# Row sums of x on TensorE, a root in halves, and single feature blocks at the head of a transformer block's kernel

## The chip, the cores and the metric

The kernel runs on one core of one Trainium2 chip. The metric is the device time of an execution in microseconds. Four executions of the kernel before are shown: three timed runs and the profiled one.

## The reference, cut to what matters

The reference computes one layer of a diffusion backbone over 256 latent tokens (x) and 256 context tokens (ctx) with 2048 features in float32. The part that matters here is its beginning:

```
mod   = silu(c) @ w_ada + b_ada            # 6 x 2048 columns, latent tokens
mod_c = silu(c_ctx) @ w_ada + b_ada        # the same for context tokens
h_lat = rmsnorm(x,   norm1_g) * (1 + sc1)  + sh1
h_ctx = rmsnorm(ctx, norm1_g) * (1 + csc1) + csh1
z     = h @ w_in                           # 8000 columns: attention q, k, v, MLA parts, gates
rmsnorm(x, g) = x * rsqrt(mean(x * x) + 1e-6) * g
lam   = exp(sum(lp[0] * lp[1])) - exp(sum(lp[2] * lp[3])) + 0.2   # used in the attention alone
```

Behind it come differential attention, multi-head latent attention, the merge of both, a SwiGLU feed-forward part and a last norm, which the change does not touch.

## The kernel before, in words

Tokens are the free dimension and features the partitions: `xnT` holds 16 k-tiles of 128 features by 512 tokens, latent tokens first. A float32 operand is split into a high part and a low part in the reduced type fp32r, written by ScalarE (a copy) and VectorE (the difference), and a product is three matmuls: high by high, high by low, low by high. In the names `hl` and `hc` stand for the modulated activations of latent and context tokens, `wh` and `wl` for weights, with two buffers each for the parts of an activation and three for each part of a weight.

**Row sums and root.** x arrives in eight units of two k-tiles. ScalarE squares a unit (L338, L341), VectorE adds it to `xsum` of 1024 columns (L342), folds that to 512 columns (L343), and TensorE multiplies by a matrix of ones (L345), which leaves each token's sum on every partition in `ps`. The function `newton` (from L323) makes the reciprocal root: Ln, Exp and Square on ScalarE (L325 to L327), a correction step of three operations on VectorE (L328 to L330). The result `rb` has a column for each token.

**Modulation, block by block.** `mod_gemv(f0, nf, order)` makes shift and scale of `nf` k-tiles from `f0` on. It first multiplies x by `rb` on VectorE (L388). Its weights `w_mod` are 2 MB a k-tile, in units of 512 KB (`sraw`, twelve buffers, L394). TensorE multiplies each of the 16 contraction tiles by 32 columns that hold c and c_ctx, four in different column groups at a time (L408, the "vector products" below; `pgb` is their bank), ScalarE copies the sums (L401), TensorE transposes them (L404), VectorE adds the four groups up (L415) and makes shift and scale (L421, L422, `modc`). Then ScalarE writes the high part of the modulated k-tile (L427), VectorE modulates in float32 (L428) and writes the low part (L429).

**First products.** `first_group` loads two parts of `w_in` for the same k-tiles (320 and 512 columns each, 832 in all; five buffers `raw`), splits them (L439 to L442, L169, L170), and puts 42 matmuls a k-tile into a list, `queue`: seven output groups by two streams by three parts. Their sums stay in seven banks (`g`, `g_x`) over all 16 k-tiles.

**The order.** TensorE's order in this stage is written by hand (`manual_schedule`). The list `order` of a call says it step by step: "g4" means four vector products, "t" the copy, eight products of the queue and the transposes, a number that many products of the queue. So the products of one block cover the vector products and the modulation of the next. The calls before are two single blocks (k-tiles 0 and 1) and seven pairs. The other engines take their work in the order of a scheduler. Weights and x come through SP's queue, in program order; the transfers share eight semaphores in turn, so each waits until the one eight places ahead (x, w_mod, w_in and the two small ones alike) has landed. The small vector operands and `da_lambda` come through ScalarE's queue. `da_lambda`'s two dot products, exponential and sum are made at the very start (L297 to L305).

Behind the stage the query, key and value projections begin, with the sums of the latent norm (L590) first.

Of the kernel before, what the change touches and what calls it, by code (L numbers as in the profile page):

```python
# [26 lines left out]
LAM_INIT = 0.8 - 0.6 * math.exp(-0.0)  # L27
# [69 lines left out]
def kernel(  # L97
# [19 lines left out]
    const, _c0 = pool("const")  # L117
    ctx.callback(_c0)
    stream, _c1 = pool("stream")
# [19 lines left out]
    def nm(s):  # L139
        uid[0] += 1  # L140
        return f"{s}{uid[0]}"
# [93 lines left out]
    def group_b(w, c0, n, nkt, toks, name, ups=2, tick=None, stagger=0):  # L235
# [41 lines left out]
    ones = const.tile([P, P], F32, name="ones")  # L277
# [10 lines left out]
    b1 = const.tile([P, 16], F32, name="b1")  # L288
    nc.vector.tensor_scalar_add(b1, bcol[:, 16:32], 1.0)

    ls = const.tile([P, 4], F32, name="ls")
    setup = stream.tile([P, 1024], F32, tag="wl", name="setup", bufs=3)
    lamb, lj = setup[:, 0:256], setup[:, 512:576]
    nc.scalar.dma_start(
        out=lamb, in_=da_lambda.rearrange("a f d -> (a f d)").partition_broadcast(P))
    for i in range(2):
        nc.vector.tensor_tensor_reduce(  # L297
            lj, lamb[:, i * 128 : i * 128 + 64], lamb[:, i * 128 + 64 : i * 128 + 128],
            op0=ALU.mult, op1=ALU.add, scale=1.0, scalar=0.0, accum_out=ls[:, i : i + 1])
    with tc.issue_after(silu.ins):  # L300
        nc.scalar.preload_act_table_set("natural_log_exp_and_others")
    nc.scalar.activation(ls[:, 0:2], ls[:, 0:2], AF.Exp)
    nlam = ls[:, 2:3]
    nc.vector.tensor_sub(nlam, ls[:, 1:2], ls[:, 0:1])
    nc.vector.tensor_scalar_add(nlam, nlam, -LAM_INIT)  # L305


    right, close_right = pool("right", side="right")
# [3 lines left out]
    xp, close_x = pool("xp", side="right")  # L312
    xnT = xp.tile([P, KT, 512], F32, name="xnT")
    c32 = xp.tile([P, KT, 32], F32, name="c32")
    nc.gpsimd.memset(c32, 0.0)
    nc.vector.tensor_copy(c32[:, :, 0:2], cols[:, 0:32].rearrange("p (v k) -> p k v", v=2))
    srp, close_sr = pool("srp", side="right")

# [4 lines left out]
    def newton(y, q, ps, n):  # L323

        nc.scalar.activation(y, ps, AF.Ln, bias=epsc, scale=1.0 / n)  # L325
        nc.scalar.activation(y, y, AF.Exp, scale=-0.5)
        nc.scalar.activation(q, y, AF.Square)  # L327
        nc.vector.scalar_tensor_tensor(q, ps, n * EPS, q, op0=ALU.add, op1=ALU.mult)  # L328
        nc.vector.tensor_scalar(q, q, -0.5 / n, 1.5, op0=ALU.mult, op1=ALU.add)
        nc.vector.tensor_mul(y, y, q)  # L330

    xsum = xp.tile([P, 1024], F32, name="xsum")
    for u in range(8):
        xu = xnT[:, 2 * u : 2 * u + 2, :]
        nc.sync.dma_start(out=xu, in_=xt[:, 2 * u : 2 * u + 2, :])
        xu = xu.rearrange("p a n -> p (a n)")
        if u == 0:
            nc.scalar.activation(xsum, xu, AF.Square)  # L338
        else:
            sq = stream.tile([P, 1024], F32, tag="wh", name=nm("sq"), bufs=3)  # L340
            nc.scalar.activation(sq, xu, AF.Square)  # L341
            nc.vector.tensor_add(xsum, xsum, sq)  # L342
    nc.vector.tensor_add(xsum[:, :512], xsum[:, :512], xsum[:, 512:])  # L343
    ps = acc(nm("ps"))
    nc.tensor.matmul(ps, ones, xsum[:, :512], start=True, stop=True)  # L345
    rb = xsum[:, :512]
    newton(rb, xsum[:, 512:], ps, D)

# [1 line left out]
    g0 = [Acc(acc(nm("g0_"))) for _ in range(4)] + [Acc(ps_s(nm("g0_"))) for _ in range(2)] + [Acc(ps_x("g0_x"))]  # L352
# [1 line left out]
    modc = xp.tile([P, KT, 2, 2], F32, name="modc")  # L354
    modr = xp.tile([P, 2, 2, 2], F32, name="modr")

    queue, last_load = [], [None]

    def pop(n):
        for f in queue[:n]:  # L360
# [22 lines left out]
    def mod_gemv(f0, nf, order):  # L383

        for kt in range(f0, f0 + nf):
            nc.vector.tensor_mul(xnT[:, kt, :], xnT[:, kt, :], rb)  # L388
        w = nf * 256
        a = 4 // nf  # L390
        vs = []
        for u in range(KT // a):
            raw = srp.tile([P, 1024], F32, tag="sraw", name=nm("sraw"), bufs=SRAW)
            last_load[0] = nc.sync.dma_start(  # L394
                out=raw, in_=w_mod.block(u * a, a, f0 * P, nf * P, D + f0 * P, nf * P))
            vs += [raw[:, i * w : (i + 1) * w] for i in range(a)]
        done = 0
        for step in order:
            if step == "t":
                res = xp.tile([P, 512], F32, tag="res", name=nm("res"), bufs=1)  # L400
                nc.scalar.copy(res[:, :w], pgb[:, :w])  # L401
                pop(8)
                for j in range(2 * nf):
                    nc.tensor.transpose(pgb[:, j * P : (j + 1) * P], res[:, j * P : (j + 1) * P], ident)  # L404
            elif isinstance(step, str):
                for kt in range(done, done + int(step[1:])):
                    j = kt % 4
                    nc.tensor.matmul(pgb[32 * j : 32 * j + 32, :w], c32[:, kt, :], vs[kt],  # L408
                                     start=kt < 4, stop=kt >= 12, tile_position=(0, 32 * j))
                done += int(step[1:])  # L410
            else:
                pop(step)
        assert done == KT

        nc.vector.tensor_reduce(  # L415
            modr[:, :, :nf, :],
            pgb[:, : 2 * nf * P].rearrange("p (s i g v) -> p s i v g", s=2, i=nf, g=4)[:, :, :, 0:2, :],
            axis=AX.X, op=ALU.add)
        for i in range(nf):
            kt = f0 + i  # L420
            nc.vector.tensor_scalar(modc[:, kt, 0, :], modr[:, 0, i, :], bcol[:, kt : kt + 1], None, op0=ALU.add)  # L421
            nc.vector.tensor_scalar(modc[:, kt, 1, :], modr[:, 1, i, :], b1[:, kt : kt + 1],  # L422
                                    n1g[:, kt : kt + 1], op0=ALU.add, op1=ALU.mult)
            for v, hh in enumerate((hl, hc)):
                sh, sc = modc[:, kt, 0, v : v + 1], modc[:, kt, 1, v : v + 1]
                xv = xnT[:, kt, v * 256 : v * 256 + 256]
                nc.scalar.activation(hh[0][:, kt, :], xv, AF.Identity, bias=sh, scale=sc)  # L427
                nc.vector.tensor_scalar(xv, xv, sc, sh, op0=ALU.mult, op1=ALU.add)  # L428
                nc.vector.tensor_sub(hh[1][:, kt, :], xv, hh[0][:, kt, :].bitcast(F32))  # L429
        queue.extend(first_group(f0, nf))  # L430

    def first_group(k0, nk):
# [41 lines left out]
        return todo  # L474

    with tc.manual_schedule(engines={mybir.EngineType.PE}):
        mod_gemv(0, 1, ["g4", "g4", "g4", "g4", "t"])
        mod_gemv(1, 1, [16, "g16", "t"])
        mod_gemv(2, 2, [36, "g8", 4, "g8", "t"])
        for f0 in range(4, KT, 2):  # L480

            mod_gemv(f0, 2, [len(queue) - 54, "g16", "t", 22])
        pop(len(queue))
    with tc.issue_after(last_load[0].ins):
        nc.sync.dma_start(out=cst, in_=consts)
# [234 lines left out]
    for i in range(2):  # L720
        sq = t512()
# [4 lines left out]
    for i in range(4):  # L726
        t = t256()
# [146 lines left out]
    for g in range(4):  # L874
# [3 lines left out]
        for j in range(2):  # L878
            for a in range(2):
                kt = g * 4 + j * 2 + a  # L880
# [156 lines left out]
```

## Time and profile before

| what | us |
|---|---|
| median of three timed runs | 1600.13 |
| lowest and highest of them | 1592.73, 1602.61 |
| the profiled execution | 1590.97 |
| its span, first to last instruction | 1589.2 |
| TensorE busy in it | 1536.9 (97%) |
| VectorE busy | 1015.8 (64%) |
| ScalarE busy | 736.8 (46%) |
| bytes moved by the 16 DMA engines | 356.34 MB, mean 224 GB/s |

The profile is one execution, recorded by hardware. PE is TensorE, DVE VectorE, ACT ScalarE, SP the engine that issues transfers. Busy time of TensorE counts the pipelined tails of its matmuls, so two that follow each other closely overlap in their durations, and starts tell more than durations. A float32 matmul is recorded as two passes. The granted clock is the share of TensorE's full speed that was granted in a stretch. A wait is put down to what came last by the profile.

### The profile page before, as it was taken

The page shows a single profiled execution, that of the slowest core. Times are in us where ns is not written, and L with a number is a line of the kernel's source. Part 1 is how long each engine was busy: PE and PEld are TensorE (multiplying, and loading weights), DVE is VectorE, ACT ScalarE, POOL GpSimd, SP SyncE. Part 2 cuts the span into 40 slices and gives each one's busy share as a digit, 9 for nine tenths or more (in the row PEclk, how much of TensorE's full clock was granted, in tenths as well). Part 3 has the DMA queues.
Part 4 walks back from the last instruction along what each step waited for, and adds up shares of the span by engine and source line. Part 5 has one row for each costly group of instructions (what it writes and reads, how often), then busy time and mean ns, then how long its engine had stood idle before and what let it go on. Part 6 is the DMA issues. An engine that isn't in the chain of part 4 may idle for free.

```text
span 1589.2 us, 28863 instructions
## 1 busy us (share of the span) xinstructions
PE 1536.9 (97%) x11966; PEld 1443.3 (91%) x11966; DVE 1015.8 (64%) x1360; ACT 736.8 (46%) x1038; POOL 16.1 (1%) x14
## 2 busy tenths in 40 slices
PE   3899999998999999999999999999999999999997
PEld 2678899998899999999999999999999999888886
DVE  5437887787896667677777566767555545455454
ACT  4335455545675444444446444444444444344343
POOL 0000000000000000000000000000000000011010
PEclk9999999999999999999999999999999999999999
DMA  9894653456454787878884668888566656665563
GB/s 369 338 366 161 210 176 111 139 176 202 150 160 162 258 280 259 291 266 296 299 280 148 229 226 300 289 271 280 196 191 196 197 192 220 194 192 197 191 193 120
DMA packets 100595, 356.34 MB, mean 224 GB/s; under 512 B 10993, under 2 KB 13553, under 8 KB 100209
## 3 DMA queue, kind: packets, MB, share of 16 engines
q1 hardware_dynamic: 99600, 351.58, 65.9%
q10 hardware_dynamic: 864, 2.93, 0.5%
q8 instruction: 93, 1.52, 0.4%
q14 instruction: 38, 0.30, 0.1%
HBM read 352.37 MB, written 2.10 MB: 223 GB/s over the span
## 4 chain that ended last, share of the span: by engine, by line
PE 72%; DMA 9%; DVE 6%; issue 1%; ACT 1%; DVEq 0%; POOLq 0%; POOL 0%; ACTq 0%
PE gate L157 15%; PE up L157 15%; PE down L157 15%; DMA raw<-in_w_ada_dram 9%; PE ga L157 4%; PE dv L157 4%; PE gb L157 3%; DVE gacc L507 3%; PE dk L157 2%; DVE wl L170 2%; PE yab L157 2%; PE wo L157 2%; PE dq L157 1%; PE cq L157 1%; PE pt L647 1%
## 5 line engine op out<-in xcount | busy, mean ns | idle before, releaser
L170 DVE TENSOR_TENSOR wl<-raw,wh 128x1024 fp32r<-128x1024 f32 (+1 forms) x453 | 548.9, 1222 | 326.9 <-ACT wh L169 312.6
L169 ACT CAST wh<-raw 128x1024 fp32r<-128x1024 f32 (+1 forms) x453 | 474.9, 1051 | 572.7 <-PE down L157 134.9
L507 DVE SCALAR_TENSOR_TENSOR gacc<-raw,cols,gacc 128x1024 f32<-128x1024 f32 x120 | 154.0, 1283 | 123.5 <-DMA raw<-in_w_ada_dram 123.2
L157 PE MATMUL gate<-h,wh 128*128 128x256 f32 x1386 | 175.9, 277 | 0.0
L157 PE MATMUL up<-h,wh 128*128 128x256 f32 x1386 | 175.8, 277 | 0.0
L157 PE MATMUL down<-wh,hid 128*128 128x512 f32 x696 | 173.3, 389 | 0.0
L157 PEld LDWEIGHTS up<-h,wh 128*128 128x128 f32 x1386 | 166.4, 188 | 0.1
L157 PEld LDWEIGHTS gate<-h,wh 128*128 128x128 f32 x1386 | 166.5, 188 | 0.0
L157 PEld LDWEIGHTS down<-wh,hid 128*128 128x128 f32 x696 | 130.7, 188 | 27.0
L157 PE MATMUL gate<-h,wl 128*128 128x256 f32 x704 | 96.7, 277 | 0.0
L157 PE MATMUL up<-h,wl 128*128 128x256 f32 x704 | 96.7, 277 | 0.0
L157 PE MATMUL down<-wl,hid 128*128 128x512 f32 x352 | 94.6, 389 | 0.0
L157 PEld LDWEIGHTS up<-h,wl 128*128 128x128 f32 x704 | 87.8, 188 | 0.2 <-DVE wl L170 0.2
L157 PEld LDWEIGHTS gate<-h,wl 128*128 128x128 f32 x704 | 87.8, 188 | 0.1
L157 PEld LDWEIGHTS down<-wl,hid 128*128 128x128 f32 x352 | 66.1, 188 | 13.7
L157 PE MATMUL ga<-hl,wh 128*128 128x256 f32 x504 | 65.6, 278 | 0.0
L157 PE MATMUL wo<-mT,wh 128*128 128x256 f32 x504 | 64.2, 278 | 0.0
L157 PE MATMUL gb<-hl,wh 128*128 128x256 f32 x504 | 64.0, 278 | 0.0
L157 PEld LDWEIGHTS ga<-hl,wh 128*128 128x128 f32 x504 | 61.4, 188 | 0.6 <-ACT wh L169 0.4
L157 PEld LDWEIGHTS wo<-mT,wh 128*128 128x128 f32 x504 | 60.6, 188 | 0.4 <-issue 0.4
L157 PEld LDWEIGHTS gb<-hl,wh 128*128 128x128 f32 x504 | 60.7, 188 | 0.0
L408 PE MATMUL pgb<-sraw,c 128*32 128x512 f32 (+1 forms) x288 | 32.8, 597 | 17.4 <-DMA sraw<-in_w_mod_dram 17.4
(334 smaller groups left out, 2316.5 us busy)
## 6 DMA issues: line engine op xcount, KB each, us to landing
raw<-in_w_ada_dram SPq DMA_DIRECT2D x128, 512.0 KB, 4.2
raw<-in_w_in_dram SPq DMA_DIRECT2D x119, 512.0 KB, 4.6
raw<-in_w_ffn_gate_dram SPq DMA_DIRECT2D x88, 512.0 KB, 4.4
raw<-in_w_ffn_up_dram SPq DMA_DIRECT2D x88, 512.0 KB, 4.4
raw<-in_w_ffn_down_dram SPq DMA_DIRECT2D x88, 512.0 KB, 3.6
sraw<-in_w_mod_dram SPq DMA_DIRECT2D x64, 512.0 KB, 8.5
raw<-in_w_out_dram SPq DMA_DIRECT2D x32, 512.0 KB, 5.1
raw<-in_w_o_da_dram SPq DMA_DIRECT2D x16, 512.0 KB, 4.8
```

What stands on the lines that cost most here:

```text
L157: nc.tensor.matmul(region, lhsT, rhs, start=False, stop=last, skip_group_check=key != self.lead)
L169: nc.scalar.copy(h, v)
L170: nc.vector.tensor_sub(l, v, h.bitcast(F32))
L408: nc.tensor.matmul(pgb[32 * j : 32 * j + 32, :w], c32[:, kt, :], vs[kt], start=kt < 4, stop=kt >= 12, tile_position=(0, 32 * j))
L507: nc.vector.scalar_tensor_tensor(a, raw, cols[:, kt : kt + 1], a, op0=ALU.mult, op1=ALU.add)
L647: nc.tensor.transpose(pt[:, j * P : (j + 1) * P], a[:, j * P : (j + 1) * P], ident)
```

## The change

Five things change in the modulation stage, and nothing behind it.

- The squares are no longer added up on VectorE. Each unit's square is folded to 512 columns (one VectorE operation), and TensorE adds the eight units by eight products with ones into the same bank. These stand in `order` as "s0" to "s7".
- `newton` runs twice, for latent and for context tokens.
- The multiplication of x by `rb` as a step of its own goes. One VectorE operation multiplies by scale and root, ScalarE adds the shift for the high part, and a second VectorE operation adds the shift and takes the high part off.
- K-tiles 0 to 11 are single blocks, the last four two pairs, with other numbers of queued products between the steps.
- Idle matmuls ("d" and a number: zeros by ones, 256 columns, into a bank whose first product overwrites it) stand ahead of the sums (12), between them (6), between the first vector products (3) and behind the first transposes (4).

Lambda's arithmetic moves to where k-tile 11's activations are done; its load stays at the start.

```diff
-    for i in range(2):
-        nc.vector.tensor_tensor_reduce(
-            lj, lamb[:, i * 128 : i * 128 + 64], lamb[:, i * 128 + 64 : i * 128 + 128],
-            op0=ALU.mult, op1=ALU.add, scale=1.0, scalar=0.0, accum_out=ls[:, i : i + 1])
+    def lambdas():
+        for i in range(2):
...
+    warm = xp.tile([P, 256], F32, name="warm")
+    nc.gpsimd.memset(warm, 0.0)
...
-    xsum = xp.tile([P, 1024], F32, name="xsum")
     for u in range(8):
-        xu = xnT[:, 2 * u : 2 * u + 2, :]
-        nc.sync.dma_start(out=xu, in_=xt[:, 2 * u : 2 * u + 2, :])
-        xu = xu.rearrange("p a n -> p (a n)")
-        if u == 0:
-            nc.scalar.activation(xsum, xu, AF.Square)
-        else:
-            sq = stream.tile([P, 1024], F32, tag="wh", name=nm("sq"), bufs=3)
-            nc.scalar.activation(sq, xu, AF.Square)
-            nc.vector.tensor_add(xsum, xsum, sq)
-    nc.vector.tensor_add(xsum[:, :512], xsum[:, :512], xsum[:, 512:])
+        nc.sync.dma_start(out=xnT[:, 2 * u : 2 * u + 2, :], in_=xt[:, 2 * u : 2 * u + 2, :])
     ps = acc(nm("ps"))
-    nc.tensor.matmul(ps, ones, xsum[:, :512], start=True, stop=True)
-    rb = xsum[:, :512]
-    newton(rb, xsum[:, 512:], ps, D)
+    rbq = xp.tile([P, 1024], F32, name="rbq")
+    rb = rbq[:, :512]
+
+    def row_sums(u):
+
+        sq = stream.tile([P, 1024], F32, tag="wh", name=nm("sq"), bufs=3)
+        nc.scalar.activation(sq, xnT[:, 2 * u : 2 * u + 2, :].rearrange("p a n -> p (a n)"), AF.Square)
+        nc.vector.tensor_add(sq[:, :512], sq[:, :512], sq[:, 512:])
+        nc.tensor.matmul(ps, ones, sq[:, :512], start=u == 0, stop=u == 7)
+        if u == 7:
+            for v in range(2):
+                cs = slice(v * 256, v * 256 + 256)
+                newton(rb[:, cs], rbq[:, 512 + v * 256 : 768 + v * 256], ps[:, cs], D)
...
-        for kt in range(f0, f0 + nf):
-            nc.vector.tensor_mul(xnT[:, kt, :], xnT[:, kt, :], rb)
...
+            elif isinstance(step, str) and step[0] == "s":
+                row_sums(int(step[1:]))
+            elif isinstance(step, str) and step[0] == "d":
+                for _ in range(int(step[1:])):
+                    nc.tensor.matmul(g0[6].t[:, :256], ones, warm, start=True, stop=True)
...
-                nc.scalar.activation(hh[0][:, kt, :], xv, AF.Identity, bias=sh, scale=sc)
-                nc.vector.tensor_scalar(xv, xv, sc, sh, op0=ALU.mult, op1=ALU.add)
-                nc.vector.tensor_sub(hh[1][:, kt, :], xv, hh[0][:, kt, :].bitcast(F32))
+                nc.vector.scalar_tensor_tensor(xv, xv, sc, rb[:, v * 256 : v * 256 + 256], op0=ALU.mult, op1=ALU.mult)
+                nc.scalar.activation(hh[0][:, kt, :], xv, AF.Identity, bias=sh)
+                made[0] = nc.vector.scalar_tensor_tensor(
+                    hh[1][:, kt, :], xv, sh, hh[0][:, kt, :].bitcast(F32), op0=ALU.add, op1=ALU.subtract)
...
-        mod_gemv(0, 1, ["g4", "g4", "g4", "g4", "t"])
-        mod_gemv(1, 1, [16, "g16", "t"])
-        mod_gemv(2, 2, [36, "g8", 4, "g8", "t"])
-        for f0 in range(4, KT, 2):
-
-            mod_gemv(f0, 2, [len(queue) - 54, "g16", "t", 22])
+        sums = []
+        for u in range(8):
+            sums += [f"s{u}", "d1" if u < 6 else "d0"]
+        mod_gemv(0, 1, ["d12"] + sums + ["g4", "d1", "g4", "d1", "g4", "d1", "g4", "t", "d4"])
+        mod_gemv(1, 1, [20, "g16", "t"])
+        mod_gemv(2, 1, [len(queue) - 34, "g16", "t"])
+
+        for f0 in range(3, 12):
+            mod_gemv(f0, 1, [len(queue) - 38, "g16", "t"])
+        with tc.issue_after(made[0].ins):
+            lambdas()
+        mod_gemv(12, 2, [len(queue) - 38, "g16", "t", 6])
+        for f0 in range(14, KT, 2):
+            mod_gemv(f0, 2, [len(queue) - 54, "g16", "t"])
```

At TensorE's start there stood, before, the product with ones behind the first vector products (`pgb` their bank, `ps` the sums, `g` the first products):

```order
L408 MATMUL pgb<-sraw_163,c_104 32x256 x4
L345 MATMUL ps_142<-xsum,ones 128x512
L408 MATMUL pgb<-sraw_165,c_104 32x256 x4
L408 MATMUL pgb<-sraw_167,c_104 32x256 x4
L408 MATMUL pgb<-sraw_169,c_104 32x256 x4
L404 MATMUL pgb<-cols,res_187 128x128 x2
L155 MATMUL g_11_153<-hl_93,wh_202 128x256
```

Now the twelve idle matmuls (`warm` by `ones`) and sums s0 to s5, each with one idle matmul behind it, come first, and it goes on with s6:

```order
L346 MATMUL ps_116<-sq_180,ones 128x512
L346 MATMUL ps_116<-sq_184,ones 128x512
L415 MATMUL pgb<-sraw_130,c_97 32x256 x4
L411 MATMUL g_x<-warm,ones 128x256
L415 MATMUL pgb<-sraw_132,c_97 32x256 x4
L411 MATMUL g_x<-warm,ones 128x256
L415 MATMUL pgb<-sraw_134,c_97 32x256 x4
L411 MATMUL g_x<-warm,ones 128x256
L415 MATMUL pgb<-sraw_136,c_97 32x256 x4
L406 MATMUL pgb<-cols,res_219 128x128 x2
L411 MATMUL g_x<-warm,ones 128x256 x4
L155 MATMUL g_4_121<-hl_86,wh_238 128x256
```

All the sums stand ahead of the first vector product, and idle matmuls stand between the vector products and behind the transposes.

On VectorE, behind the sums, the root (`xsum`) stood once over 512 columns, with other work between its steps, before the first scaling of x:

```order
L343 TENSOR_TENSOR xsum<-xsum 128x512
L328 SCALAR_TENSOR_TENSOR xsum<-ps_142,xsum 128x512
L440 TENSOR_TENSOR wl_203<-raw_200,wh_202 128x320
L329 TENSOR_SCALAR xsum<-xsum 128x512
L415 TENSOR_REDUCE modr<-pgb 128x2x2
L330 TENSOR_TENSOR xsum<-xsum 128x512
L421 TENSOR_SCALAR modc<-modr,cols 128x2
L388 TENSOR_TENSOR xnT<-xnT,xsum 128x512
```

Now both halves (`rbq`) come one behind the other, and the joint step with scale and root follows the low parts of the weights:

```order
L331 SCALAR_TENSOR_TENSOR rbq<-ps_116,rbq 128x256
L332 TENSOR_SCALAR rbq<-rbq 128x256
L333 TENSOR_TENSOR rbq<-rbq 128x256
L331 SCALAR_TENSOR_TENSOR rbq<-ps_116,rbq 128x256
L332 TENSOR_SCALAR rbq<-rbq 128x256
L333 TENSOR_TENSOR rbq<-rbq 128x256
L448 TENSOR_TENSOR wl_239<-raw_236,wh_238 128x320
L422 TENSOR_REDUCE modr<-pgb 128x2x2
L428 TENSOR_SCALAR modc<-modr,cols 128x2
L429 TENSOR_SCALAR modc<-modr,b_79,cols 128x2
L170 TENSOR_TENSOR wl_247<-raw_244,wh_246 128x512
L434 SCALAR_TENSOR_TENSOR xnT<-xnT,modc,rbq 128x256 x2
```

On ScalarE the two halves stand with these waits; the second one's Ln waits for VectorE, and the semaphore's value is that of the first half's L331:

```order
L328 ACTIVATE rbq<-ps_116,epsc 128x256 [waits PE_49]
L329 ACTIVATE rbq<-rbq 128x256 [waits Activation_49]
L330 ACTIVATE rbq<-rbq 128x256 [waits Activation_49]
L328 ACTIVATE rbq<-ps_116,epsc 128x256 [waits DVE_49]
L329 ACTIVATE rbq<-rbq 128x256 [waits Activation_49]
L330 ACTIVATE rbq<-rbq 128x256 [waits Activation_49]
L447 CAST wh_238<-raw_236 128x320 [waits DMAHW6_49]
```

So the halves overlap only in VectorE's last two steps of the first.

## Rows read from the trace of the kernel before

**Rows 1.** Windows by stage: from:to, us, busy by engine, PEclk, DMA share, GB/s.

```profile
0.00:29.76 29.76, 6.57 (x36) 2.02 (x37) 14.38 (x30) 14.92 (x22) 0.73 (x5) 1.00 0.95 356
29.76:38.00 8.24, 7.08 (x49) 4.88 (x49) 6.44 (x13) 1.80 (x5) 0.00 (x0) 0.59 1.03 410
38.00:56.00 18.00, 14.00 (x110) 10.23 (x109) 10.82 (x27) 6.20 (x12) 0.00 (x0) 1.00 0.87 333
56.00:149.06 93.06, 93.06 (x804) 76.45 (x804) 42.59 (x120) 34.80 (x67) 0.00 (x0) 1.00 0.81 306
149.06:1589.20 1440.14, 1416.15 (x10974) 1349.74 (x10972) 941.54 (x1175) 679.09 (x935) 15.39 (x9) 1.00 0.65 214
```

**Rows 2.** TensorE's waits, 29 to 60 us: us in total, times, longest.

```profile
PE g L157 <- DVE hl L429: 3.7, 3, 1.4
PE g L157 <- ACT hl L427: 1.5, 1, 1.5
```

**Rows 3.** Timeline of SP's issues (start, us), and its waits, 11 to 22 us.

```profile
16.02 0.33 SPq L394 DMA_DIRECT2D sraw<-in_w_mod_dram  x1
21.16 0.33 SPq L161 DMA_DIRECT2D raw<-in_w_in_dram  x1
21.60 0.36 SPq L394 DMA_DIRECT2D sraw<-in_w_mod_dram  x1
...
SPq L394 <- DMA xnT<-in_xt_dram: 2.8, 3, 0.9
```

**Rows 4.** Timeline of the head: start, us, engine, instruction [idle before].

```profile
16.55 1.06 ACT L341 ACTIVATE sq<-xnT 128x1024 f32<-128x1024 f32 x1 [0.27 <-DVE xsum L342]
20.54 0.69 DVE L343 TENSOR_TENSOR xsum<-xsum 128x512 f32<-128x512 f32 x1
21.29 2.08 PE L345 MATMUL ps<-xsum,ones 128*128 128x512 f32 x2 [2.79 <-DVE xsum L343]
23.40 0.69 ACT L325 ACTIVATE xsum<-ps,epsc 128x512 f32<-128x512 f32 x1 [5.79 <-PE ps L345]
25.32 0.44 ACT L439 CAST wh<-raw 128x320 fp32r<-128x320 f32 x1
26.15 0.37 ACT L401 COPY res<-pgb 128x256 f32<-128x256 f32 x1 [0.39 <-PE pgb L408]
27.46 0.68 DVE L330 TENSOR_TENSOR xsum<-xsum 128x512 f32<-128x512 f32 x1
29.76 0.38 PE L155 MATMUL g<-hl,wh 128*128 128x256 f32 x1 [2.50 <-ACT hl L427]
31.30 0.58 PE L157 MATMUL g<-hl,wh 128*128 128x256 f32 x1 [1.16 <-DVE hl L429]
32.11 0.42 PE L157 MATMUL g<-hc,wl 128*128 128x256 f32 x1
```

**Rows 5.** Two windows (PEclk before DMA share) and k-tile 1's vector products.

```profile
33.00:34.00 1.00, 1.00 (x6) 1.00 (x6) 1.00 (x3) 0.00 (x0) 0.00 (x0) 0.50 1.02 410
37.00:38.00 1.00, 1.00 (x17) 0.36 (x9) 0.00 (x0) 0.00 (x0) 0.00 (x0) 0.79 1.03 405
...
34.80 3.20 PE L408 MATMUL pgb<-sraw,c 128*32 128x256 f32 x32
```

**Rows 6.** Timeline of TensorE, 59 to 74 us.

```profile
59.45 3.64 PE L408 MATMUL pgb<-sraw,c 128*32 128x512 f32 x32
63.02 0.50 PE L157 MATMUL g<-hl,wh 128*128 128x256 f32 x2
...
73.22 2.35 PE L408 MATMUL pgb<-sraw,c 128*32 128x512 f32 x20
```

**Rows 7.** Timeline of VectorE, 64 to 69 us.

```profile
64.76 0.19 DVE L415 TENSOR_REDUCE modr<-pgb 128x8 f32<-128x32 f32 x1 [7.42 <-ACT wh L441]
...
68.80 0.42 DVE L429 TENSOR_TENSOR hl<-xnT,hl 128x256 fp32r<-128x256 f32 x1
```

**Rows 8.** Timeline of TensorE at the stage's end: four passes are two products with ones.

```profile
149.06 1.88 PE L590 MATMUL pq<-t,ones 128*128 128x512 f32 x4
```

More of the change, by code (lines that the diff above doesn't have):

```diff
@@ L289 @@
     nc.vector.tensor_scalar_add(b1, bcol[:, 16:32], 1.0)
[L291 to L295, printed above, removed]
-    for i in range(2):
-        nc.vector.tensor_tensor_reduce(
-            lj, lamb[:, i * 128 : i * 128 + 64], lamb[:, i * 128 + 64 : i * 128 + 128],
-            op0=ALU.mult, op1=ALU.add, scale=1.0, scalar=0.0, accum_out=ls[:, i : i + 1])
     with tc.issue_after(silu.ins):
         nc.scalar.preload_act_table_set("natural_log_exp_and_others")
-    nc.scalar.activation(ls[:, 0:2], ls[:, 0:2], AF.Exp)
+    ls = const.tile([P, 4], F32, name="ls")
     nlam = ls[:, 2:3]
-    nc.vector.tensor_sub(nlam, ls[:, 1:2], ls[:, 0:1])
-    nc.vector.tensor_scalar_add(nlam, nlam, -LAM_INIT)
+    def lambdas():
+        for i in range(2):
+            nc.vector.tensor_tensor_reduce(
+                lj, lamb[:, i * 128 : i * 128 + 64], lamb[:, i * 128 + 64 : i * 128 + 128],
+                op0=ALU.mult, op1=ALU.add, scale=1.0, scalar=0.0, accum_out=ls[:, i : i + 1])
+        nc.scalar.activation(ls[:, 0:2], ls[:, 0:2], AF.Exp)
+        nc.vector.tensor_sub(nlam, ls[:, 1:2], ls[:, 0:1])
+        nc.vector.tensor_scalar_add(nlam, nlam, -LAM_INIT)
     right, close_right = pool("right", side="right")
@@ L315 @@
     nc.gpsimd.memset(c32, 0.0)
+    warm = xp.tile([P, 256], F32, name="warm")
+    nc.gpsimd.memset(warm, 0.0)
+    lamb = xp.tile([P, 256], F32, name="lamb")
+    lj = xp.tile([P, 64], F32, name="lj")
+    nc.scalar.dma_start(out=lamb, in_=da_lambda.rearrange("a f d -> (a f d)").partition_broadcast(P))
     nc.vector.tensor_copy(c32[:, :, 0:2], cols[:, 0:32].rearrange("p (v k) -> p k v", v=2))
@@ L355 @@
     modr = xp.tile([P, 2, 2, 2], F32, name="modr")
-    queue, last_load = [], [None]
+    queue, last_load, made = [], [None], [None]
     def pop(n):
```

## The prediction

> **What bounds the kernel now.** I read the stages first [rows 1]: from 149.06 us to the end TensorE is busy 1416.15 of 1440.14 us, and the change touches nothing there, so what it brings must come from the modulation stage ahead of it. In that stage 56.00 to 149.06 has no idle TensorE at all; before 56 us it is busy 27.65 of 56 us. Three losses stand there. The first is the start: TensorE's first product of the stage is at 29.76, and the fifth, after which it runs on, at 32.11 [rows 4]. The second is the clock: in 33 to 34 us the granted clock is 0.50, the lower of its levels (1.2 of 2.4 GHz), and the 16 vector products of k-tile 1 last 3.20 us from 34.80 [rows 5]. The third is waiting for the modulated activations after 29 us: 3.7 us for VectorE's low parts and 1.5 us for ScalarE's high parts [rows 2]. From 56 us on the price of TensorE's work is the bound, and that work stays.
>
> **The start, step by step.** The change does not make data land sooner. SP's issues read as landings, since a transfer waits for the one eight places ahead: the last unit of x lands at 16.02, the last w_mod unit of k-tile 0 at 21.16, its first w_in part at 21.60 [rows 3]. Before, the sums were late for another reason: the last square started at 16.55, seven dependent adds followed, the folding add ended at 21.23, the product with ones took 21.29 to 23.29, and the root was ready at 28.14 [rows 4].
>
> Now: last unit 16.0, square 1.06, add of 512 columns 0.69 (the folding add's form), so 17.8. A row sum on TensorE is two passes of 512 columns. At 21.29 it took 2.0 us; at 149.06 two such sums are through in 1.88 us, 0.94 each with the tail [rows 4, 8]. I take 0.9, the price at 149.06 less a part of the tail, because the twelve idle matmuls keep TensorE at work from 1.7 us on; in the old run it worked from 31.3 without a longer pause, and the clock was up in the course of 37 to 38 us [rows 5]. An idle matmul has half the columns: 0.45. If the lower clock holds as long here, the idle ones end near 10 us; 8 x 0.9 + 6 x 0.45 = 9.9 us behind them ends at 19.9 back to back, the data allow 18.7. I take 18.9 to 19.
>
> Of the clock the granted figure before 29.76 is 1.00 [rows 1], which would make 2.0 us the full-speed price of a row sum. The pair at 149.06 speaks against it [rows 8]. The Trainium skill (TensorE: Matmul & The Clock Gate, section "Seeing it yourself") says that recorded clock events have been seen to be unreliable. By the column, eight sums and six idle ones would take 22 us and not 9.9, which is the first rival's sum; by the durations it is 9.9.
>
> The root in halves is no gain by itself: the order shows that the second half's first ScalarE step waits for VectorE, whose first step of half one reads the same sums. A half has three ScalarE steps of 256 columns, of which a copy takes 0.37 and 512 columns take up to 0.69, so 1.2 us [rows 4]; 1.2 + 0.4 + 1.2 and 1.2 on VectorE are 4.0 us against 4.74 (23.40 to 28.14). Both halves are ready at 22.9. The other chain arrives together: w_in at 21.6, cast 0.44, copy 0.37, transposes 0.3, so 22.8. Then VectorE's row: low part of w_in 0.4, reduction 0.15, two scale steps 0.45, second low part 0.65, scale and root in one 0.4, and ScalarE 0.6: first product at 25.6. The low parts of both streams follow by 26.6, the fifth product is at 26.8. Against 32.11 that is **5.3 us**; I take 5.2.
>
> **The clock.** From the fifth product at 32.11 to the vector products at 34.80 stand 12 products, 0.21 us each and the change of kind [rows 4, 5]; at the higher clock one takes 0.117 (63.02 to 73.22, 84 products and four transposes [rows 6]), so 1.15 us. The vector products at 1.85 instead of 3.2 are 1.35 us more: **2.5 us**.
>
> **The waits.** 3.7 + 1.5 less the 1.16 before 31.30, which the start contains, is 4.0 us. After the change two remain. For k-tile 1 only 14 products cover the chain behind the transposes, and ScalarE's cast of the second w_in part stands before its activations: about 0.9 us. At k-tile 12, the first pair, 30 products (3.5 us) cover a chain which lasted from the reduction at 64.76 to the first low part at 69.2 [rows 7]; the joint step saves some of it: about 1.2 us more is waited. From k-tile 2 to 11 the chain is reduction 0.15, scale steps 0.5, two joint steps 0.8, ScalarE 0.6, low part 0.45, under 3.2 us with the wait for a free weight buffer, and 26 or 30 products (3.0 to 3.5 us) cover it. Saved: **1.9 us**.
>
> **What single blocks cost.** Ten k-tiles go from pairs to single blocks. The 16 vector products of a pair take 3.57 us (59.45 to 63.02) [rows 6]; half of it is 1.79, and 256-column ones at the higher clock stand in no row. Bounds are 1.79 and 3.2, the row at mostly the lower clock. I take 1.85 plus 0.1 for one more change between kinds, since even the slow row holds no more than the columns: 0.13 a k-tile, **1.3 us** lost; ends 0.3 and 4 us, the upper one with a quarter microsecond more for each change of kind.
>
> **What costs nothing.** Sixteen scalings of x leave VectorE, 25 idle matmuls come, and ScalarE and VectorE get more, smaller operations; VectorE is busy 42.59 and ScalarE 34.80 of 93.06 us there [rows 1]. The last four idle ones end near 24.7, 0.9 us before data; without that cover each costs 0.45. Moving lambda to k-tile 11 puts about 0.8 us on two engines with that slack; its load keeps its place, so SP's queue is released as before. SP issues ten more transfers.
>
> **Sum:** 5.2 + 2.5 + 1.9 - 1.3 = **8.3 us**. The profiled execution took 1590.97 us (span 1589.2) and would take 1583. It lies 9 us below the median of the runs; from that, 1600.13, the forecast is **1592 us**, 0.5% less.
>
> **Rivals.**
> 1. *Slower: row sums queue behind idle matmuls at the low clock.* They stand in TensorE's order ahead of every sum. At 2.0 and 1.0 us, 12 x 1.0 from 1.7 us and then 22 us end at 35.7; the root comes at 39.7, the fifth product at 43.5, 11.4 us late. With 1.9 and -1.3 it is 10.8 us slower, 1611. It decides if the last sum ends after 27.7. For it: the 2.0 us row; against it: the clock came up under steady work [rows 4, 5]. Chance 0.06.
> 2. *The clock falls back between the last sum and k-tile 0*, where TensorE waits for transfers with short idle matmuls between. The 2.5 us and 0.8 for slower sums and transposes are lost, gain 5, about 1595. For it: TensorE had worked in pieces from 21.29 to 29.76, and then ran slow [rows 4, 5]. Chance 0.13.
> 3. *Transfers starve TensorE.* A k-tile needs 2.52 MB (w_mod and 832 columns of w_in) in 7.0 us, 360 GB/s; the queue delivered 410 in 29.76 to 38, with single-block transfers in it, and 333 in 38 to 56, then held back by buffers [rows 1]. At 333 each of eleven k-tiles takes 0.57 us longer: gain 2, 1598. Chance 0.1. The Trainium skill (DMA: Bandwidth & Descriptors, section "Bandwidth") asks for transfers of 1 MiB and gives each some 2.0 us fixed: as an estimate, ten more are 20 us if none overlap, 1611. The 410 GB/s row does not bear that out.
> 4. *More than forecast*: no wait at k-tiles 1 and 12, single blocks at half price, the start 0.8 us sooner: 12.5 us, 1588. Chance 0.13.
>
> The forecast itself keeps 0.58. The four executions shown spread from 1590.97 to 1602.61, so each case carries some 6 us either way; with the unknown 0.3 to 4 us the range is **1579 to 1603**. About 1% (16 us) is what a measurement tells from no change. No case alone gains 16, but the median before lies high among its runs, and one new median near its low end adds 7 to 9 us to 8.3 or 12.5: faster by over 1% has 0.22, within 1% 0.74, slower 0.04, most of it the first rival.
>
> **What would show it.** Right: row sums of 0.9 us with the last one ending near 19; first product near 25.6; 0.12 us a product from there; two waits of about 1 us at k-tiles 1 and 12; vector products of 1.8 to 1.95 us; the stage's end near 140 instead of 149.06 and nothing moved behind it. Wrong: sums of 2 us, a granted clock of 0.50 after 25 us, waits for w_mod or at every k-tile, or a stage behind it that grows.

## The result: 0.5% slower, and the profile after

The changed kernel takes 1599.33 us (median of 20 runs, 1594.58 to 1610.39). The kernel before takes 1591.23, the median of 20 runs; the three shown ahead of the prediction are among them, and their median of 1600.13 was high. The ratio (this kernel's time by that of the kernel before) is 1.0052, 95% interval 1.0035 to 1.0068. The forecast was 1592 us, 0.5% faster. That 1599.33 lies inside its range of 1579 to 1603 is luck: the forecast took its 8.3 us off a base 9 us too high. Taken off 1591.23 they give 1583, 16 us less than was measured. The profiled execution has a span of 1597.7 us against 1589.2, with a mean granted clock of 0.988 against 0.994.

The stage itself came out nearly as forecast. Windows by stage of the changed kernel, in the columns of [rows 1]; the second begins at the first product, the last at the stage's end:

```profile
0.00:26.60 26.60, 23.96 (x100) 14.70 (x100) 10.83 (x28) 15.95 (x24) 0.98 (x6) 1.00 0.94 349
26.60:38.00 11.40, 10.76 (x108) 8.28 (x112) 4.82 (x12) 3.46 (x9) 0.00 (x0) 1.00 1.03 405
38.00:56.00 18.00, 18.00 (x190) 15.35 (x183) 8.60 (x24) 7.35 (x20) 0.00 (x0) 1.00 1.03 401
56.00:141.35 85.35, 84.82 (x827) 71.40 (x826) 45.10 (x124) 33.45 (x81) 0.00 (x0) 1.00 0.84 320
141.35:1597.70 1456.35, 1423.32 (x10974) 1357.53 (x10972) 942.95 (x1177) 680.22 (x935) 15.41 (x9) 0.99 0.64 211
```

The stage ends at 141.35 instead of 149.06, 7.7 us earlier. What follows lasts 1456.35 us instead of 1440.14, 16.2 us longer, and the number of TensorE's instructions in it (x10974) is the same. Most of the loss, 10.7 us by the table below, stands directly behind the stage. TensorE's waits there in the changed kernel, 141 to 210 us:

```profile
PE dq L157 <- DVE wl L170: 7.9, 1, 7.9
PE ps L692 <- ACT t L658: 2.6, 1, 2.6
```

And in the kernel before, 149 to 210 us:

```profile
PE ps L676 <- ACT t L642: 1.9, 1, 1.9
PE dq L157 <- DVE wl L170: 1.6, 2, 1.5
PE dv L155 <- DVE t L594: 0.6, 1, 0.6
```

TensorE needs the low part of the weights of `dq`'s second unit (the queries of pair 0; the attention takes its heads in four pairs, and `dq` comes in four units of 512 KB). VectorE in the kernel before, 154 to 156 us, and TensorE's row that waited for it:

```profile
153.95 0.42 DVE L548 TENSOR_TENSOR dk<-r,dk 64x256 fp32r<-64x256 f32 x1
154.40 1.23 DVE L170 TENSOR_TENSOR wl<-raw,wh 128x1024 fp32r<-128x1024 f32 x1
155.65 0.69 DVE L328 SCALAR_TENSOR_TENSOR t<-pq,t 128x512 f32<-128x512 f32 x1
...
155.68 1.19 PE L157 MATMUL dq<-hl,wl 128*128 128x256 f32 x8 [0.18 <-DVE wl L170]
```

The same places in the changed kernel, with ScalarE's cast of that unit ahead of them:

```profile
139.50 1.05 ACT L169 CAST wh<-raw 128x1024 fp32r<-128x1024 f32 x1
...
147.50 0.69 DVE L331 SCALAR_TENSOR_TENSOR t<-pq,t 128x512 f32<-128x512 f32 x1
...
153.94 0.42 DVE L564 TENSOR_TENSOR dk<-r,dk 64x256 fp32r<-64x256 f32 x1
154.39 4.67 DVE L170 TENSOR_TENSOR wl<-raw,wh 128x1024 fp32r<-128x1024 f32 x4
...
155.67 2.07 PE L157 MATMUL dq<-hl,wl 128*128 128x256 f32 x8 [7.88 <-DVE wl L170]
```

Before, the row L170 stood in the middle of the evacuation (the emptying of the stage's banks: pair 0's and 1's keys `dk`, the latent `ckvn`), ahead of the latent's root steps (L328). Now it stands behind all of it, with three more of its kind. Its input was ready at 140.55, when ScalarE's cast ended; VectorE came to it at 154.39. An engine takes its rows in order here, so one row behind 20 us of evacuation (134.28 to 154.39 us) holds TensorE. The Trainium skill says the same of VectorE and ScalarE, "strict FIFO" (TensorE: Matmul & The Clock Gate, section "Architectural detail: the array is 16× 32×32, not 1× 128×128"); the row agrees.

The wait costs more than itself. Windows of the changed kernel behind the stage:

```profile
141.35:147.80 6.45, 6.44 (x46) 5.28 (x44) 6.20 (x19) 5.90 (x13) 0.00 (x0) 1.00 0.01 4
147.80:155.67 7.87, 0.00 (x1) 0.00 (x1) 7.59 (x14) 3.39 (x6) 0.00 (x0) 0.66 0.00 0
155.67:164.38 8.71, 8.71 (x56) 8.71 (x57) 6.47 (x6) 2.76 (x3) 0.00 (x0) 0.72 0.84 288
164.38:186.14 21.76, 21.76 (x194) 21.76 (x193) 14.42 (x25) 7.88 (x13) 0.00 (x0) 1.00 0.58 202
186.14:200.00 13.86, 11.23 (x62) 10.39 (x61) 9.35 (x15) 6.49 (x14) 0.00 (x0) 0.75 0.46 148
```

While TensorE idles, the granted clock falls; from 152 to 160 us it is 0.50, the lower level, and eight products take 2.07 us, where they took 1.19 before (last rows of the two VectorE fences above). Hardly any data moves either (4 and 0 GB/s), but that alone is no difference: before, too, it is 0 GB/s from 149.06 to 155.69. From 186 us there is a second loss. VectorE in the changed kernel, and TensorE's row:

```profile
192.17 1.22 DVE L170 TENSOR_TENSOR wl<-raw,wh 128x1024 fp32r<-128x1024 f32 x1
194.67 1.23 DVE L170 TENSOR_TENSOR wl<-raw,wh 128x1024 fp32r<-128x1024 f32 x1 [1.28 <-issue]
195.82 0.16 DVE L698 RECIPROCAL c<-c 128x2 f32<-128x2 f32 x1
...
191.86 0.80 PE L692 MATMUL ps<-dk,dq 128*128 128x512 f32 x1 [2.63 <-ACT t L658]
```

The kernel before, TensorE's row and the window from the first scores to 200 us:

```profile
192.22 0.50 PE L676 MATMUL ps<-dk,dq 128*128 128x512 f32 x1 [1.91 <-ACT t L642]
...
186.52:200.00 13.48, 11.57 (x87) 10.78 (x86) 12.32 (x21) 9.02 (x20) 0.00 (x0) 1.00 0.57 171
```

Two low parts of pair 1 stand ahead of the first softmax's reciprocal; before, that reciprocal came at 193.82, 7.3 us behind the first scores, now 9.7 us behind them. TensorE waits only 0.7 us longer, but its granted clock falls, 0.75 against 1.00 in the windows to 200 us. From the first scores to pair 1's values it comes to 24.3 us instead of 20.9. What the two rows and what the clock have of these 3.4 us was not separated.

Where TensorE begins a piece of work, read from its timelines (us; "old" and "new" name the order behind the stage, "stretch" is from the stage's end to pair 1's values):

| | before | changed | changed, 2nd profile | changed stage, old order | old stage, new order | one row moved | one constraint |
|---|---|---|---|---|---|---|---|
| stage's end (`pq`) | 149.06 | 141.35 | 141.20 | 141.47 | 147.51 | 141.48 | 141.63 |
| first scores (`ps`) | 186.52 | 186.14 | 185.96 | 180.44 | 191.52 | 184.47 | 179.65 |
| pair 1's values (`dv`) | 207.38 | 210.40 | 210.38 | 199.61 | 215.30 | 208.35 | 200.06 |
| **stretch** | **58.32** | **69.05** | **69.18** | **58.14** | **67.79** | **66.87** | **58.43** |
| gates (`ga`) | 468.78 | 472.58 | 472.32 | 460.51 | 478.23 | 470.16 | 461.24 |
| feed-forward (`gate`) | 855.27 | 863.10 | 862.51 | 853.20 | 868.87 | 860.68 | 850.61 |

The 7.7 us are ahead at the stage's end, spent by the first scores, and 3.0 us behind at pair 1's values. 4.0 us more go between the gates and the feed-forward; the last experiments are about those.

### The profile page after: what moved, and what is told of

Same layout as the page of the kernel before. It is cut to its first block, busy times and chain, and to the rows that moved or that the text cites. A ratio compares the mean times of both kernels' runs of the same rounds, so it can differ in the third digit from the quotient of the medians.

```text
span 1597.7 us, 29393 instructions
## 1 busy us (share of the span) xinstructions
PE 1560.9 (98%) x12190; PEld 1467.3 (92%) x12190; DVE 1012.3 (63%) x1362; ACT 740.4 (46%) x1066; POOL 16.4 (1%) x15
## 4 chain that ended last, share of the span: by engine, by line
PE 72%; DMA 10%; DVE 6%; issue 1%; ACT 1%; DVEq 0%; POOLq 0%; POOL 0%; ACTq 0%; SPq 0%
PE gate L157 15%; PE up L157 15%; PE down L157 15%; DMA raw<-in_w_ada_dram 9%; PE dv L157 3%; DVE gacc L523 3%; PE ga L157 3%; PE wo L157 3%; PE gb L157 2%; PE dk L157 2%; PE yab L157 2%; PE dq L157 2%; DVE wl L170 2%; PE cq L157 1%; PE pt L663 1%
## 5 line engine op out<-in xcount | busy, mean ns | idle before, releaser
L170 DVE TENSOR_TENSOR wl<-raw,wh 128x1024 fp32r<-128x1024 f32 (+1 forms) x458 | 549.6, 1209 | 331.4 <-ACT wh L169 316.7
L157 PE MATMUL g<-hl,wh 128*128 128x256 f32 x186 | 39.1, 287 | 1.2 <-DVE hl L436 0.5
```

The lines of the kernel that those rows point to most:

```text
L157: nc.tensor.matmul(region, lhsT, rhs, start=False, stop=last, skip_group_check=key != self.lead)
L170: nc.vector.tensor_sub(l, v, h.bitcast(F32))
```

## The experiments

**The order swapped both ways.** Behind the stage the two programs have the same instructions, and the same order on every engine but for 120 places in a row on VectorE, 72 on ScalarE and 427 on TensorE; TensorE's order is written by hand in the stage alone. So the order can be set without any other change: each instruction gets an edge to the one that is to stand ahead of it (issue order, no wait). The numbers count instructions from the load of the constants.

```diff
+BEHIND_DVE = "51 53 80-81 91 82 86 92 84 93 107 94 96 108-109 98 110 100 155 66 102 67 ..."
...
+def issue_in_order(tc, orders, cst):
+    made = {i.name: i for i in tc.nc.cur_bb.bb.instructions}
+    first = int(cst.name.split("-")[1])
...
+        for was, now in zip(names, names[1:]):
+            tc.add_manual_dep(made[now], was, info, reason="order")
...
+    issue_in_order(tc, (BEHIND_DVE, BEHIND_ACT, BEHIND_PE,), cst_load.ins)
```

The changed kernel with the old order:

> The changed kernel, with the order in which VectorE, ScalarE and TensorE issue the work behind the modulation stage (120, 72 and 427 instructions) set to what it was in the kernel before. Theory A (the order behind the stage eats the gain): the stage ends at 141.4 us as in the changed kernel, no wait of TensorE for dq's low parts over 2 us, first scores near 179 us instead of 186, and a time 8 us below the kernel before, about 1583 (ratio 0.995). Rival B (the evacuation of the stage's banks or the transfers bound what follows, whatever the order): first scores near 186 us, time as before, 1591. Rival C (something that the new stage leaves behind, its clock or its buffers, slows what follows): 1599 as the changed kernel.

1588.87 us against 1593.83 before; ratio 0.9970, interval 0.9946 to 0.9994: faster. TensorE's rows with a wait, 141 to 190 us (lines of these kernels stand 21 further on):

```profile
148.75 1.20 PE L178 MATMUL dq<-hl,wl 128*128 128x256 f32 x8 [0.84 <-DVE wl L191]
152.79 0.39 PE L176 MATMUL dv<-wh,hc 128*128 128x256 f32 x1 [0.57 <-DVE t L631]
156.90 1.21 PE L178 MATMUL dq<-hl,wl 128*128 128x256 f32 x8 [1.37 <-DVE wl L191]
184.42 0.50 PE L713 MATMUL ps<-dk,dq 128*128 128x512 f32 x1 [0.28 <-ACT t L679]
```

The wait of 7.9 us is now 0.84 (1.37 at the last unit), the second loss is 0.28, and pair 1's values begin 7.8 us earlier than before: theory A. B fails on the first scores (180.44, not 186), C on the time. The time that A named, 1583, was missed by 6 us; only 5.0 of the 7.8 us are in the median.

The kernel before with the new order:

> The kernel before, stage untouched, with the order of the changed kernel behind the stage on VectorE, ScalarE and TensorE. Theory A: TensorE waits 7 to 8 us for dq's low parts near 155 us, its clock falls to 0.5 there, the values of pair 1 begin 10.7 us later than at 207.4, and the kernel takes about 1602 (ratio 1.007). Rivals B and C: the order costs nothing by itself, 1591.

1602.74 us, ratio 1.0059 (1.0031 to 1.0087). The wait is there in a kernel whose stage is untouched:

```profile
161.48 2.07 PE L178 MATMUL dq<-hl,wl 128*128 128x256 f32 x8 [7.53 <-DVE wl L191]
```

So the order alone costs 0.6% with the old stage, and with the new stage it makes the difference between 0.3% faster and 0.5% slower. The stretch is 58.1 to 58.4 us with the old order and 67.8 to 69.2 with the new one, whichever stage is ahead. In this profile the old stage ended at 147.51, 1.55 us sooner than in the first one, with no change to it: the first product came 0.5 us sooner, and the granted clock was 1.00 from 36 us on, where it had been 0.50 until 37. Against this execution the changed stage is 6.2 us ahead and not 7.7; the changed stage, with either order, ended at 141.2 to 141.6 in all seven profiles.

**One row.** The changed kernel's own order on all engines, with VectorE's row for unit 1 put back:

```diff
-98 66 102 67 112 68 ... 118 155 185 215      (VectorE, numbers of instructions; 155 is dq's unit 1)
+98 155 66 102 67 112 68 ... 118 185 215
```

> The changed kernel with its own order behind the stage, but one VectorE row moved: the low part of dq's second unit stands where it stood before, ahead of the latent's three root steps. If this row is the whole cause: the wait of 7.9 us goes, first scores near 179 us, time about 1592 (the later loss of 3.4 us stays). If TensorE's order, which now takes all four dq units ahead of the values, matters as well: the wait moves to the third unit, whose low part still stands behind the evacuation (about 156.8 us against a need at 151.3, so 5.4 us), first scores near 183.5 us, time about 1597.

1598.55 us, ratio 1.0029 (1.0004 to 1.0054). TensorE:

```profile
148.58 1.18 PE L178 MATMUL dq<-hl,wl 128*128 128x256 f32 x8 [0.67 <-DVE wl L191]
156.74 2.08 PE L178 MATMUL dq<-hl,wl 128*128 128x256 f32 x8 [5.16 <-DVE wl L191]
```

The row is not the whole cause, though nothing but its place had held it: VectorE does it at 147.30 now. The wait moves to the third unit, at 156.74. In the old order TensorE had a part of pair 0's values between those units to work on; in the new one it takes all four units first. The two engines' orders fit each other, and a row moved on one of them does not restore the fit.

**One constraint, the rest left to the scheduler.**

```diff
+BEHIND_DVE = "155 66"
...
+    issue_in_order(tc, (BEHIND_DVE,), cst_load.ins)
```

> The changed kernel with a single constraint: on VectorE the low part of dq's second unit is issued ahead of the latent's root steps; all else is left to the scheduler, which then puts VectorE, ScalarE and TensorE nearly in the order of the kernel before (11, 6 and 34 of 1177, 890 and 10928 places differ). If the order is the cause, this one line does what the whole old order did: longest wait for dq under 2 us, first scores near 180.4 us, values of pair 1 near 199.6, time 1588 to 1590 against 1593. If the places that still differ matter: the wait stays above 4 us, time 1596 or more.

1590.70 us, ratio 0.9988 (0.9963 to 1.0014), stretch 58.43. One edge brings the whole old order back but for a few places, TensorE's too. The ratio is below 1, but its interval holds 1, so the time alone shows no gain; the stretch does.

**An order of our own.**

```diff
-51 53 80-81 91 82 86 92 84 93 107 94 96 ... 155 66 ... 185 215 283
+51 53 80-82 155 86 84 66-68 70 74 185 215 91-94 96 100 98 102 72 76 283
```

The minus line is the old order. The lists of ScalarE and TensorE are others, too; TensorE takes all four `dq` units first, as in the new order.

> The changed kernel with an order of our own behind the stage: VectorE's low parts of dq's units 1 to 3 ahead of most of the evacuation (unit 1 behind the first two key blocks, units 2 and 3 behind the latent's scaling), the latent's root steps ahead of pair 1's keys on ScalarE and VectorE, and on TensorE all four dq units ahead of the values. If the order of VectorE is what TensorE waits for: the waits of 0.8, 0.6 and 1.4 us that stay with the old order go, first scores near 177.6 us instead of 180.4, time 3 us below the run with the old order, about 1586 against 1593 to 1594 before (ratio 0.995). Rival: VectorE, busy 4.8 of 5 us from 141 to 160, is the bound itself, so the waits only move: first scores at 180 to 182, time as with the old order.

1591.54 us, ratio 0.9995 (0.9972 to 1.0017). The waits for `dq` are gone, and another one came:

```profile
153.02 1.07 PE L178 MATMUL dq<-hl,wl 128*128 128x256 f32 x8
155.84 0.39 PE L176 MATMUL dv<-wh,hl 128*128 128x256 f32 x1 [1.76 <-ACT wh L190]
```

ScalarE's cast of the values' first unit stood behind pair 1's keys in our list, and for those ScalarE had waited 4.5 us for VectorE. First scores come at 180.11, no better than with the old order: the wait moved, as the rival said. Whether VectorE is the bound, or only that place of the cast, was not tested.

**Parts of the change**, each with the old order behind the stage, so that the stage's end tells what the part is worth. Without the idle matmuls, all 25 of them (the expectation says 24):

```diff
-            sums += [f"s{u}", "d1" if u < 6 else "d0"]
-        mod_gemv(0, 1, ["d12"] + sums + ["g4", "d1", "g4", "d1", "g4", "d1", "g4", "t", "d4"])
+            sums += [f"s{u}"]
+        mod_gemv(0, 1, sums + ["g4", "g4", "g4", "g4", "t"])
```

> As the first kernel of this set (old order behind the stage), without any of the 24 idle matmuls. If they hold the clock up: row sums of about 2 us at first, the last one ends 1 to 5 us after 19.2, the granted clock or the products of k-tiles 0 and 1 are at half speed, the stage ends at 143 to 146 us, time 2 to 5 us above that kernel, 1585 to 1588. If the sums alone keep TensorE at the higher clock: last sum at 19.2, stage end at 141.4, time 1583.

1590.03 us, ratio 0.9969 (0.9947 to 0.9991); stage's end 143.51. TensorE's first product and two windows:

```profile
26.84 0.58 PE L176 MATMUL g<-hl,wh 128*128 128x256 f32 x1 [2.66 <-ACT hl L456]
...
24.00:28.00 4.00, 1.34 (x6) 0.93 (x5) 3.49 (x10) 1.75 (x5) 0.00 (x0) 0.68 1.03 400
28.00:32.00 4.00, 4.00 (x22) 3.69 (x25) 0.49 (x1) 0.46 (x2) 0.00 (x0) 0.50 1.02 407
```

The first product comes at 26.84 against 26.85 with them, so they do nothing for the start; behind it the granted clock is 0.50 until 32 us, and the stage ends 2.0 us later. In the total they cannot be told from nothing (0.9969 against 0.9970 with them).

Pairs from k-tile 2 on:

```diff
-        for f0 in range(3, 12):
-            mod_gemv(f0, 1, [len(queue) - 38, "g16", "t"])
+        mod_gemv(2, 2, [36, "g8", 4, "g8", "t"])
+        for f0 in range(4, KT, 2):
+            mod_gemv(f0, 2, [len(queue) - 54, "g16", "t", 22])
```

> As the first kernel of the first set (changed stage, old order behind it), but with the feature blocks of one k-tile for k-tiles 0 and 1 alone and pairs from 2 on, as before the change. If single blocks cost what the prediction said (1.3 us for ten) and save most of the waits (1.9): the stage ends at 141.5 to 143 us against 141.5. If pairs wait for their larger transfers and longer chains as before (1.15, 1.50 and 1.35 us near 42 to 56 us): 143 to 145. If single blocks only cost: 140.2. Time follows the stage's end, 1588 to 1592.

1595.19 us, ratio 1.0005 (0.9981 to 1.0030). The stage ends at 142.82, 1.35 later, with two waits back, and behind them the granted clock falls to 0.57:

```profile
46.62 0.38 PE L178 MATMUL g<-hl,wh 128*128 128x256 f32 x1 [1.40 <-ACT hl L456]
47.90 0.38 PE L178 MATMUL g<-hl,wh 128*128 128x256 f32 x1 [0.90 <-DVE hl L457]
...
48.00:52.00 4.00, 4.00 (x20) 3.90 (x21) 1.91 (x5) 0.91 (x2) 0.00 (x0) 0.57 1.03 404
```

From the first product to the stage's end TensorE idles 2.80 us here and 1.16 with single blocks, 1.64 more; the stretch itself is 116.11 us against 114.62, 1.49 more.

The squares summed on VectorE again, and the root in one piece:

```diff
-        nc.vector.tensor_add(sq[:, :512], sq[:, :512], sq[:, 512:])
-        nc.tensor.matmul(ps, ones, sq[:, :512], start=u == 0, stop=u == 7)
+            nc.vector.tensor_add(rbq, rbq, sq)
+        if u == 7:
+            nc.vector.tensor_add(rbq[:, :512], rbq[:, :512], rbq[:, 512:])
+            nc.tensor.matmul(ps, ones, rbq[:, :512], start=True, stop=True)
+            newton(rb, rbq[:, 512:], ps, D)
```

> As the first kernel of the first set, but the squares are summed on VectorE over all units, folded, and summed over partitions by one product, with the root in one piece, as before the change; the idle matmuls stay, now all ahead of that product. By the prediction's step for the start: product at 21.3, root at 27 to 28, first product of the stage at 29 to 30 instead of 26.6, and TensorE idle from 10 to 21 us, so the clock is down again for the first products: stage end 145 to 147 us, time 1592 to 1594, 4 to 5 us above the run with the old order. If the row sums bring nothing, since w_mod's transfers set the first product: 26.6 and 141.5 us.

1591.68 us, ratio 0.9992 (0.9963 to 1.0021); first product at 29.34, stage's end 144.30, 2.8 us later. That is less than the 145 to 147 expected. After 7.5 us without work the product with ones took 2.07 us, but behind it the vector products, with seven idle matmuls between and after them (the other 18 had run ahead of it), had the clock back before the first product of the stage:

```profile
20.00:24.00 4.00, 4.00 (x20) 0.86 (x18) 0.42 (x1) 2.40 (x5) 0.00 (x0) 0.57 1.03 402
24.00:28.00 4.00, 3.51 (x30) 1.78 (x27) 2.57 (x8) 1.17 (x4) 0.00 (x0) 1.00 1.03 400
```

**What is lost later.** The changed kernel once more, and the one with the old order once more:

> The changed kernel as it is, for a second profile beside the others. If the order of VectorE, which is fixed in the program, makes the wait: TensorE waits 7.9 us for dq near 148 to 156 us again and first scores come near 186 us. If the 4.1 us that were lost from 759 to 863 us belong to that one execution: that stretch (99.7 us before, 103.8 after) takes another time now; if they belong to the change, 103.8 again. Time 1599.

> The first kernel of the first set once more, for a second profile. If the gain of 7.8 us that it had up to 508 us, and of which 2.1 were left at 863 us, is lost by the program: the stretch from the gates' start (460.5) to the feed-forward (853.2), 392.7 us, takes 392 to 393 us again, against 386.5 before. If single executions differ there: another time, anywhere from 384 to 393. Time 1589.

1601.40 us, ratio 1.0050 (1.0032 to 1.0069), and 1587.23, ratio 0.9966 (0.9937 to 0.9994). The first repeats the wait (7.87 us) and the stretch (69.18) to 0.2 us. It also repeats the later loss (from the output projection's start to the feed-forward 103.0 us, in the first profile 103.8, in the kernel before 99.7). But the changed stage with the old order takes nearly as long: 102.7 and 102.4 us in its two profiles, 102.5 with the one constraint, though 99.1 without idle matmuls; and the old stage with the new order takes 102.2. From the gates' start to the feed-forward the executions took 384.3 to 395.4 us, in programs that are the same there. Much of it is one wait, as two of them show. VectorE and TensorE in the changed kernel, and VectorE in the kernel without idle matmuls:

```profile
809.58 1.29 DVE L523 SCALAR_TENSOR_TENSOR gacc<-raw,cols,gacc 128x1024 f32<-128x1024 f32 x1 [4.00 <-DMA raw<-in_w_ada_dram]
...
813.44 2.08 PE L157 MATMUL wo<-mT,wl 128*128 128x256 f32 x8 [3.12 <-DVE wl L170]
```

```profile
798.61 1.28 DVE L544 SCALAR_TENSOR_TENSOR gacc<-raw,cols,gacc 128x1024 f32<-128x1024 f32 x1 [2.60 <-DMA raw<-in_w_ada_dram]
```

In the first a transfer of w_ada was issued at 802.55, and the row that waited for it started 7.0 us later; in the other kernel 792.99 and 5.6. VectorE waits for it ahead of the low part that TensorE needs. Whether a program's timing makes that transfer late, or chance does, stays open; the order behind the stage is not what does it, since 102.7 and 99.1 both come with the old order.

## Why the prediction was wrong, step by step

- **The step that failed** is the first paragraph's: from the stage's end on "the change touches nothing there", and its sequel, "the stage's end near 140 instead of 149.06 and nothing moved behind it". The change writes nothing there, but the order there is made anew by the scheduler. The changed program's order has the L170 rows behind the whole evacuation; the prediction argued from it up to the stage's end alone. Put in the sum's terms, the work behind the stage was a term put at nothing; in the stretch to pair 1's values it measured 10.7 us lost. Swapping the order shows that this is the cause: 58 against 68 to 69 us for the stretch, in both stages. Why the scheduler chose so was not tested; that one edge turns it back shows that its choice hung on little.
- "A stage behind it that grows" was among what would make the prediction wrong, but no rival carried it: each of the four ends with the modulation stage. The chance of 0.04 was for slower by more than 1%; the measured 0.5% falls under "within 1%", 0.74, together with the forecast gain.
- **The start**, forecast 5.2: the fifth product is at 27.75 instead of 32.11 [rows 4], 4.4 us. Row sums were forecast at 0.9 us with the last one ending near 19. The first sum, the idle matmul behind it, and the end of the chain:

```profile
9.46 1.02 PE L346 MATMUL ps<-sq,ones 128*128 128x512 f32 x2
10.32 0.59 PE L411 MATMUL g_x<-warm,ones 128*128 128x256 f32 x2
...
17.20 1.99 PE L346 MATMUL ps<-sq,ones 128*128 128x512 f32 x4
19.12 0.64 PE L415 MATMUL pgb<-sraw,c 128*32 128x256 f32 x8
26.60 0.38 PE L155 MATMUL g<-hl,wh 128*128 128x256 f32 x1 [0.59 <-ACT hl L435]
27.75 0.29 PE L157 MATMUL g<-hc,wl 128*128 128x256 f32 x1
29.73 1.93 PE L415 MATMUL pgb<-sraw,c 128*32 128x256 f32 x32
```

  A sum takes 0.86 us from its start to the next one (9.46 to 10.32), and the last two are through at 19.2. That the column of 1.00 was not to be believed ahead of 29.76 held: 0.86 us a sum here, 2.0 in [rows 4], the same 1.00 in both. The root was 0.8 us later than forecast (23.7): its halves took 4.5 us and not 4.0, and the last sum ended 0.2 to 0.3 us later.
- **The clock**, forecast 2.5, measured 2.4: the granted clock is 1.00 from the first product on. The vector products last 1.93 us instead of 3.20 [rows 5], and the 16 products from 27.75 to 29.73 take 0.124 us each instead of 0.21, which saves 1.1 us on the 12 of the prediction.
- **The waits**, forecast to fall by 1.9, leaving 0.9 and 1.2: 0.37 and 0.53 are left, at k-tiles 1 and 12.
- **Single blocks**, forecast to cost 1.3: their vector products take 1.87 us from the first start to the next product, as taken (1.85). The prediction's own terms (1.85 and 0.1 against 1.79) come to 0.11 or 0.16 us a k-tile, as the 0.1 is counted for two blocks or for one, and not to 0.13. In the run with pairs 1.64 us of idle time came back, and the lower clock from 48 to 52 us cost some 1.7 (20 products in 4.0 us, at 0.117 each 2.3); together 3.3 us, where the stretch grew by 1.49. So, as an estimate, single blocks cost 1.8 us, and are still worth it.
- **Sum of the stage**: 7.7 measured, 8.3 forecast. Start 4.4, clock 2.4 and waits 3.1 (4.0 less 0.9) come to 9.9, so 2.2 were lost where 1.3 was forecast; by the estimate above all but 0.4 of them are the single blocks' price. The first rival's 2 us sums, the second's fall of the clock and the third's starved TensorE did not come (401 to 405 GB/s from 26.60 to 56 us). The third rival quoted the Trainium skill for some 2.0 us fixed per transfer, as an estimate 20 us for ten if none overlap. The Trainium skill (DMA: Bandwidth & Descriptors, section "Anatomy of one DMA — SWDGE (gpsimd) path") gives these 2.0 us for transfers that GpSimd issues. Here SP issues them, and the ten more cost no such time: the stage ended within 0.6 us of its forecast gain.
- **What a gain of the stage is worth** at the end is less sure than the stage: 7.8 us at pair 1's values with the old order, 5.0 and 5.4 in the two medians. The stage of the kernel before is itself known to no better than 1.55 us (149.06 and 147.51), and with it the start, clock and wait terms above.

## What to carry to other kernels

Where a scheduler orders the engines, an edit changes the order of code that it does not touch: compare the order of every engine to the program's end, and where a row that another engine waits for has changed places, price it like a step of the change. A gain ahead of such a place counts only when the order behind it is held; here one edge did it. A low part that only needs its load should not stand behind a long evacuation that nobody awaits yet, but the other engines' orders have to fit: with one row moved, and with an order of our own, the wait went to another place.

## What the hardware showed that was not expected

Matmuls ran at two prices with a granted clock of 1.00. Windows of TensorE at full work in the same stretch of one program (old order, second and first profile):

```profile
1110.00:1330.00 220.00, 220.00 (x1870) 220.00 (x1869) 107.70 (x98) 93.19 (x98) 0.00 (x0) 1.00 0.57 186
```

```profile
1110.00:1330.00 220.00, 220.00 (x1944) 220.00 (x1943) 111.05 (x101) 95.78 (x102) 0.00 (x0) 1.00 0.58 194
```

1870 products against 1944 in the same 220 us, 3.8% fewer, with no wait. It is not a matter of records left out: the same gate and up projections took 497.3 us instead of 485.1. Stretches of this kind stood at other places in other profiles; the execution with the dearer one took 1599.88 us and the other 1589.56, so some of the spread of the runs comes from there. What sets the price was not found.

Hardly any data moved for 14 us behind the stage (4 and 0 GB/s from 141.35 to 155.67 us in the changed kernel). SP's longest wait there, 20.9 us, ends with VectorE's L170, which gives a load's buffer back; in the kernel before the same wait is 13.9 us. So a late VectorE row also holds the next transfers, here 7.0 us longer.
